# A bf16 matmul with scale and add on one core: a semaphore for each transfer, programs without loops, another order of transfers, and the weight cast on its way in

## The chip, the core and the metric

The kernel runs on one core of a Trainium2 chip. The metric is the time on the device in microseconds (us) of one execution. A core has a tensor engine (PE), a vector engine (DVE), a scalar engine (ACT), GpSimd (POOL) and SyncE (SP), each with its own program, which wait for one another by semaphores; 16 DMA engines carry data between HBM and the on-chip memory. A transfer adds 16 to its semaphore when it is complete. Matrix products go to an accumulator memory (`mm`).

## The reference

```python
batch, m, k, n = 16, 512, 1024, 768
x: (16, 512, 1024) float32, weight: (1024, 768) float32, scale = 0.1, add_value: (16, 512, 768) float32
return (scale * np.matmul(x, weight) + add_value).astype(np.float32)
```

With the batch flattened, x has 8192 rows: 33.55 MB of x, 3.15 MB of weight and 25.17 MB of add_value are read, and 25.17 MB are written.

## The kernel before, in words

The 8192 rows are cut into T = 64 tiles of 128 rows. With G = 8 (L9), a group is 1024 consecutive rows, partition p of the chip's memory holds 8 consecutive rows of it, and tile t of a group is row t of each partition (L53 to L55). So a transfer of n tiles is, for each of the 128 partitions, one contiguous run of n rows: 4 KB a tile for x, 3 KB a tile for add_value and out.

Buffers: `xs` holds 16 tiles of x in fp32; `ao` 32 tiles of add_value, in which the result is formed and from which it is stored; `w_bf` the weight in bf16; `va` two buffers of four tiles of x in bf16; `xt` four tiles after the transpose; `mm` four accumulators.

Each tile goes through five steps:

- **SP** issues all transfers on its one queue, in the order of the list `STREAM` (L19): ("x", 8, 4) loads tiles 8 to 11 of x, "w" half of the weight, "a" add_value, "o" stores out. `sync_engine` (L87) walks the list; where a buffer must first come free, SP waits ahead of the issue, and all that follows in the list waits with it. An x load waits until ACT and POOL have moved the tiles whose slots it takes (`by_act`, `by_pool`, L109). The loads of add_value share one semaphore `a_sem`, so each of them waits until the one before has landed (L117); four tiles at 52 have `a_late`. A load into a slot from which an earlier result is stored waits for that store (L122), a store for DVE's results (`made`, L133). The entry "m" (L97) makes four transfers of under 2 KB into a tile that nothing reads. The last store, tiles 56 to 63, is issued after all engines are through (L225).
- **ACT and POOL** (`mover`, L139) cast x from fp32 to bf16 into `va`, a move of four tiles at a time, each engine half of the partitions' data in 8 instructions (L152). A move waits for its load and until the turns of the move two before are done (`turned`). The 16 moves are a hardware loop of four rounds of four.
- **DVE** (`vector_engine`, L155) first casts the two halves of the weight, which were loaded as fp32 into `ao`, into `w_bf` (`cast_w`, L158). Then for each pair of tiles it transposes (`turn`, L162) from `va` into `xt`, and later does `finish` (L172): ao = mm * scale + ao, both tiles of the pair in one instruction. The order is turn 0, turn 1, then finish p, turn p + 2, and so on, in a hardware loop over groups. `turn` waits for both movers, `finish` for the products (`done`) and, at the start of a group, for add_value.
- **PE** (`tensor_engine`, L198) waits for the whole weight (`casts`, L202) before anything else, then multiplies: for each tile 16 matmuls, 8 blocks of k by two pieces of n (512 and 256 columns), in a hardware loop over four tiles. A pair waits for its turn and for an accumulator that has been read. 32 pairs are 1024 matmuls.

The weight stands second and third in `STREAM`, right behind the first four tiles of x.

Of the kernel before, what the change touches and what calls it, by code (L numbers as in the profile page):

```python
# [6 lines left out]

P = 128
G = 8  # L9
X_SLOTS = 16  # L10
A_SLOTS = 32
CUT = 512
MM_BUFS = 4
XT_TILES = 4
VA_BUFS = 2
MOVE = 4
AHEAD = 4

STREAM = [  # L19
# [5 lines left out]
]  # L25
LAST = (56, 8)
MARKS = [15, 8, 7, 1]


@with_exitstack  # L30
def kernel(
# [8 lines left out]
    nc = tc.nc  # L40
# [6 lines left out]
    M, K = x_f.shape  # L47
    _, N = weight.shape
    T = M // P
    KC = K // (2 * P)  # L50
    KJ = 2 * KC

# [5 lines left out]
    def rows(view, s, n):  # L58
# [10 lines left out]
    xt = const.tile([P, XT_TILES, KC, P], fp32, name="xt")  # L69
    mm = psum.tile([P, MM_BUFS, 1024], fp32, name="mm")  # L70

    marks = const.tile([P, len(MARKS), 16 * len(MARKS)], fp32, name="marks")
    mark = tc.alloc_semaphore("mark")
    w_sem = [tc.alloc_semaphore(f"w{i}") for i in range(2)]
    x_sem = [tc.alloc_semaphore(f"x{i}") for i in range(X_SLOTS // MOVE)]
    a_sem, a_late = (tc.alloc_semaphore(n) for n in ("a", "a_late"))
    o_sem = [tc.alloc_semaphore(f"o{i}") for i in range(2)]
    by_act, by_pool, pool_go, turned, casts, done, made = (
        tc.alloc_semaphore(name)
        for name in ("by_act", "by_pool", "pool_go", "turned", "casts", "done", "made"))  # L80
    TURNED = MOVE * VA_BUFS
    MADE = TURNED + 2 + MM_BUFS - 2

    def slot(t):
        return (t + G) % A_SLOTS

    def sync_engine(eng):  # L87
        loads, stores, known = [], [], {}

        def need(sem, value):  # L90
            if known.get(sem, 0) < value:
                eng.wait_ge(sem, value)  # L92
                known[sem] = value

        for op, s, n in STREAM:
            last = s + n - 1
            if op == "m":  # L97
                for i, k in enumerate(MARKS):
                    eng.dma_start(marks[0:k, i, 0:16 * (i + 1)],  # L99
                                  w_v[0:k, 0, 0:16 * (i + 1)]).then_inc(mark, 16)  # L100
                continue
            if op == "w":
                dst = ao[:, s:s + n, :].rearrange("p (c r) n -> p c (r n)", r=2)
                move, sem = eng.dma_start(dst, w_v[:, s // 2:(s + n) // 2, :]), w_sem[s // 4]  # L104
            elif op == "x":
                k = s % X_SLOTS
                if last >= X_SLOTS:
                    moved = 8 * (last + 1 - X_SLOTS) // MOVE
                    need(by_act, moved)  # L109
                    need(by_pool, moved)  # L110
                    if n == 2 * MOVE:
                        eng.sem_inc(x_sem[k // MOVE + 1], 16)  # L112
                move = eng.dma_start(xs[:, k:k + n, :], rows(x_v, s, n))  # L113
                sem = x_sem[k // MOVE]
            elif op == "a":
                if loads:
                    need(a_sem, 16 * len(loads))  # L117
                if slot(s) == 0:
                    need(casts, KJ)
                if s >= A_SLOTS:  # L120
                    i = next(j for j, (a, b) in enumerate(stores) if a <= s - A_SLOTS < a + b)
                    need(o_sem[i % 2], 16 * (i // 2 + 1))  # L122
                move = eng.dma_start(ao[:, slot(s):slot(s) + n, :], rows(add_v, s, n))  # L123
                if s % G:
                    sem = a_late
                else:
                    sem = a_sem
                    loads.append((s, n))
            else:
                i = len(stores)  # L130
                if i > 1:
                    need(o_sem[i % 2], 16 * (i // 2))
                need(made, MADE + last + 1)  # L133
                move = eng.dma_start(rows(out_v, s, n), ao[:, slot(s):slot(s) + n, :])
                sem = o_sem[i % 2]
                stores.append((s, n))
            move.then_inc(sem, 16)

    def mover(eng, copy, parity, count, go=None):  # L139
        if go is None:  # L140
            eng.preload_act_table(mybir.ActivationFunctionType.Copy)  # L141
        with eng.Fori(16, 16 * (T // X_SLOTS) + 1, 16) as i:
            for q in range(X_SLOTS // MOVE):
                eng.wait_ge(x_sem[q], i)
                eng.wait_ge(turned, i + (4 * q - 12) if q < 3 else i)  # L145
                if go is not None:
                    eng.sem_inc(go, 1)  # L147
                k = MOVE * q
                src = xs[:, k:k + MOVE, :].rearrange("p i (c b k) -> p (i c) b k", b=4, k=64)
                for a in (parity, parity + 2):  # L150
                    for b in range(4):
                        copy(va[q % VA_BUFS][32 * b:32 * b + 32, :, a, :],  # L152
                             src[32 * a:32 * a + 32, :, b, :]).then_inc(count, 1)

    def vector_engine(eng):  # L155
        ao_g = ao.rearrange("p (g t) n -> p g t n", t=G)

        def cast_w(s, n):  # L158
            eng.wait_ge(w_sem[s // 4], 16)
            eng.tensor_copy(w_bf[:, s:s + n, :], ao[:, s:s + n, :]).then_inc(casts, n)  # L160

        def turn(move, half, moves=None):  # L162
            if half == 0:
                eng.wait_ge(by_act, moves)
                eng.wait_ge(by_pool, moves)
            q = 2 * half * KC
            eng.transpose(  # L167
                xt[:, 2 * half:2 * half + 2, :, :].rearrange("p i c m -> p (i c m)"),
                va[move % VA_BUFS][:, q:q + 2 * KC, :, :].bitcast(fp32).rearrange("p c a k -> p (c a k)"),
            ).then_inc(turned, 2)  # L170

        def finish(pair, at, products):  # L172
            eng.wait_ge(done, products)
            a = ao_g[:, at, 2 * pair:2 * pair + 2, :]
            q = 2 * (pair % 2)
            eng.scalar_tensor_tensor(  # L176
                a, mm[:, q:q + 2, 0:N], float(scale), a,
                op0=mybir.AluOpType.mult, op1=mybir.AluOpType.add).then_inc(made, 2)

        def group(i, at, last):  # L180
            eng.wait_ge(a_sem, i)
            for p in range(4):
                if p == 2 and not last:
                    eng.wait_ge(a_late, i)
                finish(p, at, i + (4 * p - 12) if p < 3 else i)
                if p < 2 or not last:
                    turn(1 if p < 2 else 0, p % 2, i + 8 if p == 2 else i)

        cast_w(0, 4)
        cast_w(4, 4)  # L190
        turn(0, 0, 8)
        turn(0, 1)
        with eng.Fori(16, 2 * T, 16) as i:
            group(i, bass.ds((i // 16) % (A_SLOTS // G), 1), False)
        s = slot(T - G) // G
        group(2 * T, slice(s, s + 1), True)

    def tensor_engine(eng):  # L198
        eng.sem_inc(turned, TURNED)
        eng.sem_inc(made, MADE)  # L200
        eng.sem_inc(a_late, 16 * (T // G - 2))
        eng.wait_ge(casts, KJ)  # L202
        with eng.Fori(TURNED + 2, TURNED + 2 + T, XT_TILES) as i:
            for q in range(XT_TILES):
                if q % 2 == 0:
                    eng.wait_ge(turned, i + q if q else i)
                    eng.wait_ge(made, i + q if q else i)
                for j in range(KJ):
                    x2 = xt[:, q, j // 2, :].bitcast(bf16).rearrange("p (m r) -> p r m", r=2)
                    for n0, n1 in ((0, CUT), (CUT, N)):  # L210
                        m = eng.matmul(  # L211
                            mm[:, q, n0:n1], x2[:, j % 2, :], w_bf[:, j, n0:n1],
                            start=(j == 0), stop=(j == KJ - 1))
                if q % 2:
                    m.then_inc(done, 4)
        eng.wait_ge(mark, 16 * len(MARKS))

    with tc.tile_critical(no_gpsimd_drain=True):  # L218
        sync_engine(nc.sync)
# [1 line left out]
        mover(nc.gpsimd, nc.gpsimd.tensor_copy, 1, by_pool, pool_go)  # L221
        vector_engine(nc.vector)
        tensor_engine(nc.tensor)
    s, n = LAST
    nc.sync.dma_start(rows(out_v, s, n), ao[:, slot(s):slot(s) + n, :])  # L225


# [33 lines left out]
```

## Time and profile before

| what | us |
|---|---|
| median of 3 runs (lowest, highest) | 215.4 (215.06, 215.68) |
| profiled execution, first to last instruction (its span) | 213.8 |
| PE busy with matmuls | 172.2 |
| ACT, POOL busy | 134.7, 135.4 |
| DVE busy | 97.9 |

The profiled execution's own time is known as its span; what lies around the span is the rest to the run's time.

How to read the rows: a row of the timeline or of the chain begins with the start from the span's beginning and a length, both in us; then come the engine (SPq is SP's queue of instructions), the line of the kernel and the operation, written as output<-input, with the number of instructions xN; in square brackets stands how long the engine had been idle before, and what released it. A row of a group of instructions has, after the bars, the busy time and the mean of one in nanoseconds, then the idle time before them. A row by stretch gives the busy time of each engine with the number of instructions in brackets. The granted clock is a share of TensorE's full clock.

### The profile page before, as it was taken

The numbers are of one execution on the slowest core, as the hardware profiler recorded it, in microseconds if no ns is written. First come the engines' busy times: TensorE is split into PE (matmuls) and PEld (weight loads), VectorE is DVE, ScalarE is ACT, GpSimd is POOL, SyncE is SP. The second block draws the span as 40 slices with busy tenths as digits, with TensorE's granted clock in tenths as the row PEclk, the third lists the DMA queues.
The fourth block names the chain that finished last, engine by engine and source line by source line (L and its number), as shares of the span: only waits on it lengthen the run. The fifth ranks groups of instructions, "written<-read, shape, count | busy, mean of one in ns | idle before, by whom it ended". The sixth has DMA issues, their size and how long they took to land.

```text
span 213.8 us, 2747 instructions
## 1 busy us (share of the span) xinstructions
PE 172.2 (81%) x1024; PEld 101.7 (48%) x1024; DVE 97.9 (46%) x66; ACT 134.7 (63%) x129; POOL 135.4 (63%) x132
## 2 busy tenths in 40 slices
PE   0000999999999999999999999999989906999800
PEld 0000455656566665656566665656546503556400
DVE  0046245565537555555555555555454307055310
ACT  2492947993799999896932999199900599600000
POOL 0398957994699999996932999199910499700000
PEclk9999999999999999999999999999999975799965
DMA  6999999999999999999999999999849999999766
GB/s 233 409 437 441 441 395 463 432 451 417 428 455 392 447 435 392 463 395 441 437 418 438 443 458 423 418 437 432 382 149 434 435 432 368 441 437 432 308 294 294
DMA packets 4782, 87.04 MB, mean 407 GB/s; under 512 B 558, under 2 KB 558, under 8 KB 1070
## 3 DMA queue, kind: packets, MB, share of 16 engines
q1 hardware_dynamic: 4782, 87.04, 96.1%
HBM read 61.87 MB, written 25.17 MB: 407 GB/s over the span
## 4 chain that ended last, share of the span: by engine, by line
DMA 63%; POOL 15%; PE 11%; issue 2%; SPq 2%; DVE 1%; POOLq 0%; DVEq 0%
DMA out_dram<-ao 26%; DMA xs<-in_x_dram 25%; POOL va L152 15%; DMA ao<-in_add_value_dram 12%; PE mm L211 11%; DVE ao L176 1%; SPq L99 1%; DVE xt L167 1%; SPq L113 0%; SPq L104 0%; SPq L123 0%; POOLq L145 0%; SPq L112 0%; POOLq L147 0%; SPq L92 0%
## 5 line engine op out<-in xcount | busy, mean ns | idle before, releaser
L211 PE MATMUL mm<-w_bf,xt 128*128 128x512 bf16 (+1 forms) x1024 | 172.2, 332 | 29.9 <-DVE xt L167 29.9
L152 POOL CAST va<-xs 32x1024 bf16<-32x1024 f32 x128 | 135.2, 1056 | 50.1 <-DMA xs<-in_x_dram 41.4
L152 ACT CAST va<-xs 32x1024 bf16<-32x1024 f32 x128 | 133.5, 1043 | 49.6 <-DMA xs<-in_x_dram 44.0
L211 PEld LDWEIGHTS mm<-w_bf,xt 128*128 128x128 bf16 x1024 | 101.7, 100 | 100.0 <-DVE xt L167 30.6
L176 DVE SCALAR_TENSOR_TENSOR ao<-mm,ao 128x1536 f32 (+1 forms) x32 | 56.2, 1756 | 77.7 <-PE mm L211 72.7
L167 DVE STREAM_TRANSPOSE xt<-va 128x1024 f32<-128x1024 f32 x32 | 39.5, 1235 | 14.7 <-POOL va L152 14.7
L160 DVE CAST w_bf<-ao 128x3072 bf16<-128x3072 f32 x2 | 4.5, 2228 | 13.7 <-DMA ao<-in_weight_dram 13.7
L141 ACT ACT_TABLE_LOAD x1 | 1.3, 1283 | 0.9 <-SPq L218 0.9
L242 POOL MEMSET const-float32-0.0<- 128x1 f32 x1 | 0.1, 98 | 0.2 <-issue 0.2
L242 POOL MEMSET const-bfloat16-1.0<- 128x1 bf16 x1 | 0.1, 100 | 0.0
L242 POOL MEMSET const-float32-1.0<- 128x1 f32 x1 | 0.1, 98 | 0.0
L242 POOL MEMSET const-uint8-127<- 128x1 uint8 x1 | 0.1, 98 | 0.0
## 6 DMA issues: line engine op xcount, KB each, us to landing
out_dram<-ao SPq DMA_DIRECT2D x8, 3072.0 KB, 29.3
ao<-in_add_value_dram SPq DMA_DIRECT2D x7, 3072.0 KB, 17.1
xs<-in_x_dram SPq DMA_DIRECT2D x8, 2048.0 KB, 18.8
xs<-in_x_dram SPq DMA_DIRECT2D x4, 4096.0 KB, 23.1
ao<-in_weight_dram SPq DMA_DIRECT2D x2, 1536.0 KB, 12.4
ao<-in_add_value_dram SPq DMA_DIRECT2D x2, 1536.0 KB, 8.7
marks<-in_weight_dram SPq DMA_DIRECT2D x1, 0.9 KB
marks<-in_weight_dram SPq DMA_DIRECT2D x1, 1.0 KB
```

What stands on the lines that cost most here:

```text
L99: eng.dma_start(marks[0:k, i, 0:16 * (i + 1)], w_v[0:k, 0, 0:16 * (i + 1)]).then_inc(mark, 16)
L141: eng.preload_act_table(mybir.ActivationFunctionType.Copy)
L152: copy(va[q % VA_BUFS][32 * b:32 * b + 32, :, a, :], src[32 * a:32 * a + 32, :, b, :]).then_inc(count, 1)
L160: eng.tensor_copy(w_bf[:, s:s + n, :], ao[:, s:s + n, :]).then_inc(casts, n)
L167: eng.transpose(xt[:, 2 * half:2 * half + 2, :, :].rearrange("p i c m -> p (i c m)"), va[move % VA_BUFS][:, q:q + 2 * KC, :, :].bitcast(fp ...
L176: eng.scalar_tensor_tensor(a, mm[:, q:q + 2, 0:N], float(scale), a, op0=mybir.AluOpType.mult, op1=mybir.AluOpType.add).then_inc(made, 2)
L211: m = eng.matmul(mm[:, q, n0:n1], x2[:, j % 2, :], w_bf[:, j, n0:n1], start=(j == 0), stop=(j == KJ - 1))
L242: nc = _bacc.Bacc("TRN2", target_bir_lowering=False, num_devices=1)
```

## The change

- The list becomes a string: "x4+8" loads tiles 4 to 11 of x. Each transfer but the last has its own semaphore (`landed`), and whoever needs the data waits for the transfers that carry it (`carriers`). SP waits for moves, for stores out of slots that a load takes, and for results; it no longer waits for a load.
- G is 16: partitions hold 16 consecutive rows of a group of 2048, and a transfer of 16 tiles is possible. The new order has x in transfers of eight tiles but for two, one load of add_value and one store with 16 tiles, and a last store of four tiles (60 to 63).
- The weight leaves `STREAM`. GpSimd issues two transfers, ahead of all its casts, that read fp32 and write bf16 into `w_bf`. DVE's casts go; PE waits for the two transfers. `ao` no longer holds the weight, so slots are counted from 0.
- The four small transfers "m" go.
- ACT, POOL and DVE have their programs written out in place of the loops; a wait that an earlier wait of the same engine covers is left out. PE keeps its loop.

```diff
@@ -6,7 +6,7 @@
 from concourse._compat import with_exitstack
 
 P = 128
-G = 8
+G = 16
 X_SLOTS = 16
 A_SLOTS = 32
 CUT = 512
@@ -14,17 +14,17 @@
 XT_TILES = 4
 VA_BUFS = 2
 MOVE = 4
-AHEAD = 4
-
-STREAM = [
-    ("x", 0, 4), ("w", 0, 4), ("w", 4, 4), ("x", 4, 4), ("a", 0, 8),
-    ("x", 8, 4), ("x", 12, 4), ("a", 8, 8), ("x", 16, 8), ("a", 16, 8), ("x", 24, 8),
-    ("a", 24, 8), ("x", 32, 8), ("m", 0, 4), ("o", 0, 8), ("o", 8, 8), ("a", 32, 8), ("x", 40, 4),
-    ("x", 44, 4), ("a", 40, 8), ("x", 48, 8), ("o", 16, 8), ("o", 24, 8), ("a", 48, 4), ("a", 52, 4),
-    ("x", 56, 4), ("x", 60, 4), ("a", 56, 8), ("o", 32, 8), ("o", 40, 8), ("o", 48, 8),
-]
-LAST = (56, 8)
-MARKS = [15, 8, 7, 1]
+
+STREAM = """
+    x0+4 x4+8 a0+8 a8+8 x12+4 x16+8 a16+16 x24+8 o0+8 x32+8 o8+8 a32+8 x40+8 a40+8 x48+8
+    o16+8 o24+8 a48+4 x56+8 a52+4 a56+8 o32+16 o48+4 o52+8 o60+4
+"""
+
+
+def transfers():
+    for word in STREAM.split():
+        s, n = word[1:].split("+")
+        yield word[0], int(s), int(n)
 
 
 @with_exitstack
@@ -47,6 +47,7 @@
     M, K = x_f.shape
     _, N = weight.shape
     T = M // P
+    MOVES = T // MOVE
     KC = K // (2 * P)
     KJ = 2 * KC
 
@@ -69,137 +70,119 @@
     xt = const.tile([P, XT_TILES, KC, P], fp32, name="xt")
     mm = psum.tile([P, MM_BUFS, 1024], fp32, name="mm")
 
-    marks = const.tile([P, len(MARKS), 16 * len(MARKS)], fp32, name="marks")
-    mark = tc.alloc_semaphore("mark")
+    stream = list(transfers())
+    landed = [tc.alloc_semaphore(f"{op}{s}") for op, s, n in stream[:-1]]
     w_sem = [tc.alloc_semaphore(f"w{i}") for i in range(2)]
-    x_sem = [tc.alloc_semaphore(f"x{i}") for i in range(X_SLOTS // MOVE)]
-    a_sem, a_late = (tc.alloc_semaphore(n) for n in ("a", "a_late"))
-    o_sem = [tc.alloc_semaphore(f"o{i}") for i in range(2)]
-    by_act, by_pool, pool_go, turned, casts, done, made = (
+    by_act, by_pool, pool_go, turned, done, made = (
         tc.alloc_semaphore(name)
-        for name in ("by_act", "by_pool", "pool_go", "turned", "casts", "done", "made"))
+        for name in ("by_act", "by_pool", "pool_go", "turned", "done", "made"))
     TURNED = MOVE * VA_BUFS
-    MADE = TURNED + 2 + MM_BUFS - 2
-
-    def slot(t):
-        return (t + G) % A_SLOTS
+    MADE = TURNED + MM_BUFS
+
+    def carriers(op, s, n):
+        return [sem for (o, a, k), sem in zip(stream, landed)
+                if o == op and a < s + n and s < a + k]
+
+    def slots(op, s, n):
+        ring = X_SLOTS if op == "x" else A_SLOTS
+        k = s % ring
+        assert k + n <= ring
+        return slice(k, k + n)
+
+    def engine(eng):
+        known = {}
+
+        def need(sem, value):
+            if known.get(sem.num if hasattr(sem, "num") else id(sem), 0) < value:
+                eng.wait_ge(sem, value)
+                known[sem.num if hasattr(sem, "num") else id(sem)] = value
+
+        return need
+
+    def transfer(eng, op, s, n):
+        if op == "x":
+            return eng.dma_start(xs[:, slots(op, s, n), :], rows(x_v, s, n))
+        if op == "a":
+            return eng.dma_start(ao[:, slots(op, s, n), :], rows(add_v, s, n))
+        return eng.dma_start(rows(out_v, s, n), ao[:, slots(op, s, n), :])
 
     def sync_engine(eng):
-        loads, stores, known = [], [], {}
-
-        def need(sem, value):
-            if known.get(sem, 0) < value:
-                eng.wait_ge(sem, value)
-                known[sem] = value
-
-        for op, s, n in STREAM:
-            last = s + n - 1
-            if op == "m":
-                for i, k in enumerate(MARKS):
-                    eng.dma_start(marks[0:k, i, 0:16 * (i + 1)],
-                                  w_v[0:k, 0, 0:16 * (i + 1)]).then_inc(mark, 16)
-                continue
-            if op == "w":
-                dst = ao[:, s:s + n, :].rearrange("p (c r) n -> p c (r n)", r=2)
-                move, sem = eng.dma_start(dst, w_v[:, s // 2:(s + n) // 2, :]), w_sem[s // 4]
-            elif op == "x":
-                k = s % X_SLOTS
-                if last >= X_SLOTS:
-                    moved = 8 * (last + 1 - X_SLOTS) // MOVE
-                    need(by_act, moved)
-                    need(by_pool, moved)
-                    if n == 2 * MOVE:
-                        eng.sem_inc(x_sem[k // MOVE + 1], 16)
-                move = eng.dma_start(xs[:, k:k + n, :], rows(x_v, s, n))
-                sem = x_sem[k // MOVE]
-            elif op == "a":
-                if loads:
-                    need(a_sem, 16 * len(loads))
-                if slot(s) == 0:
-                    need(casts, KJ)
+        need = engine(eng)
+        for (op, s, n), sem in zip(stream, landed):
+            last = s + n
+            if op == "x" and last > X_SLOTS:
+                moved = 8 * -(-(last - X_SLOTS) // MOVE)
+                need(by_act, moved)
+                need(by_pool, moved)
+            if op == "a":
                 if s >= A_SLOTS:
-                    i = next(j for j, (a, b) in enumerate(stores) if a <= s - A_SLOTS < a + b)
-                    need(o_sem[i % 2], 16 * (i // 2 + 1))
-                move = eng.dma_start(ao[:, slot(s):slot(s) + n, :], rows(add_v, s, n))
-                if s % G:
-                    sem = a_late
-                else:
-                    sem = a_sem
-                    loads.append((s, n))
-            else:
-                i = len(stores)
-                if i > 1:
-                    need(o_sem[i % 2], 16 * (i // 2))
-                need(made, MADE + last + 1)
-                move = eng.dma_start(rows(out_v, s, n), ao[:, slot(s):slot(s) + n, :])
-                sem = o_sem[i % 2]
-                stores.append((s, n))
-            move.then_inc(sem, 16)
+                    for old in carriers("o", s - A_SLOTS, n):
+                        need(old, 16)
+            if op == "o":
+                need(made, MADE + last)
+            transfer(eng, op, s, n).then_inc(sem, 16)
 
     def mover(eng, copy, parity, count, go=None):
+        need = engine(eng)
         if go is None:
             eng.preload_act_table(mybir.ActivationFunctionType.Copy)
-        with eng.Fori(16, 16 * (T // X_SLOTS) + 1, 16) as i:
-            for q in range(X_SLOTS // MOVE):
-                eng.wait_ge(x_sem[q], i)
-                eng.wait_ge(turned, i + (4 * q - 12) if q < 3 else i)
-                if go is not None:
-                    eng.sem_inc(go, 1)
-                k = MOVE * q
-                src = xs[:, k:k + MOVE, :].rearrange("p i (c b k) -> p (i c) b k", b=4, k=64)
-                for a in (parity, parity + 2):
-                    for b in range(4):
-                        copy(va[q % VA_BUFS][32 * b:32 * b + 32, :, a, :],
-                             src[32 * a:32 * a + 32, :, b, :]).then_inc(count, 1)
+        else:
+            half = KC // len(w_sem)
+            for i, sem in enumerate(w_sem):
+                eng.dma_start(
+                    w_bf[:, 2 * half * i:2 * half * (i + 1), :].rearrange("p (c r) n -> p c (r n)", r=2),
+                    w_v[:, half * i:half * (i + 1), :]).then_inc(sem, 16)
+        for q in range(MOVES):
+            for sem in carriers("x", MOVE * q, MOVE):
+                need(sem, 16)
+            if q >= VA_BUFS:
+                need(turned, TURNED + MOVE * (q - VA_BUFS + 1))
+            if go is not None:
+                eng.sem_inc(go, 1)
+            k = MOVE * q % X_SLOTS
+            src = xs[:, k:k + MOVE, :].rearrange("p i (c b k) -> p (i c) b k", b=4, k=64)
+            for a in (parity, parity + 2):
+                for b in range(4):
+                    copy(va[q % VA_BUFS][32 * b:32 * b + 32, :, a, :],
+                         src[32 * a:32 * a + 32, :, b, :]).then_inc(count, 1)
 
     def vector_engine(eng):
-        ao_g = ao.rearrange("p (g t) n -> p g t n", t=G)
-
-        def cast_w(s, n):
-            eng.wait_ge(w_sem[s // 4], 16)
-            eng.tensor_copy(w_bf[:, s:s + n, :], ao[:, s:s + n, :]).then_inc(casts, n)
-
-        def turn(move, half, moves=None):
-            if half == 0:
-                eng.wait_ge(by_act, moves)
-                eng.wait_ge(by_pool, moves)
+        need = engine(eng)
+
+        def turn(pair):
+            move, half = divmod(pair, 2)
+            need(by_act, 8 * (move + 1))
+            need(by_pool, 8 * (move + 1))
+            if pair > 1:
+                need(done, 4 * (pair - 1))
             q = 2 * half * KC
             eng.transpose(
                 xt[:, 2 * half:2 * half + 2, :, :].rearrange("p i c m -> p (i c m)"),
                 va[move % VA_BUFS][:, q:q + 2 * KC, :, :].bitcast(fp32).rearrange("p c a k -> p (c a k)"),
             ).then_inc(turned, 2)
 
-        def finish(pair, at, products):
-            eng.wait_ge(done, products)
-            a = ao_g[:, at, 2 * pair:2 * pair + 2, :]
+        def finish(pair):
+            for sem in carriers("a", 2 * pair, 2):
+                need(sem, 16)
+            need(done, 4 * (pair + 1))
+            a = ao[:, slots("a", 2 * pair, 2), :]
             q = 2 * (pair % 2)
             eng.scalar_tensor_tensor(
                 a, mm[:, q:q + 2, 0:N], float(scale), a,
                 op0=mybir.AluOpType.mult, op1=mybir.AluOpType.add).then_inc(made, 2)
 
-        def group(i, at, last):
-            eng.wait_ge(a_sem, i)
-            for p in range(4):
-                if p == 2 and not last:
-                    eng.wait_ge(a_late, i)
-                finish(p, at, i + (4 * p - 12) if p < 3 else i)
-                if p < 2 or not last:
-                    turn(1 if p < 2 else 0, p % 2, i + 8 if p == 2 else i)
-
-        cast_w(0, 4)
-        cast_w(4, 4)
-        turn(0, 0, 8)
-        turn(0, 1)
-        with eng.Fori(16, 2 * T, 16) as i:
-            group(i, bass.ds((i // 16) % (A_SLOTS // G), 1), False)
-        s = slot(T - G) // G
-        group(2 * T, slice(s, s + 1), True)
+        turn(0)
+        turn(1)
+        for pair in range(T // 2):
+            finish(pair)
+            if pair + 2 < T // 2:
+                turn(pair + 2)
 
     def tensor_engine(eng):
         eng.sem_inc(turned, TURNED)
         eng.sem_inc(made, MADE)
-        eng.sem_inc(a_late, 16 * (T // G - 2))
-        eng.wait_ge(casts, KJ)
+        for sem in w_sem:
+            eng.wait_ge(sem, 16)
         with eng.Fori(TURNED + 2, TURNED + 2 + T, XT_TILES) as i:
             for q in range(XT_TILES):
                 if q % 2 == 0:
@@ -213,7 +196,6 @@
                             start=(j == 0), stop=(j == KJ - 1))
                 if q % 2:
                     m.then_inc(done, 4)
-        eng.wait_ge(mark, 16 * len(MARKS))
 
     with tc.tile_critical(no_gpsimd_drain=True):
         sync_engine(nc.sync)
@@ -221,8 +203,7 @@
         mover(nc.gpsimd, nc.gpsimd.tensor_copy, 1, by_pool, pool_go)
         vector_engine(nc.vector)
         tensor_engine(nc.tensor)
-    s, n = LAST
-    nc.sync.dma_start(rows(out_v, s, n), ao[:, slot(s):slot(s) + n, :])
+    transfer(nc.sync, *stream[-1])
 
 
 # ---- launch: one core; inputs and outputs as the reference has them ----
```

## The prediction

> **What bounds the kernel now.** I read the page first (span, busy time, DMA queue, chain), then the busy time by stretch, then the chain and the timeline at the start and at the end.
>
> ```profile
> span 213.8 us, 2747 instructions
> PE 172.2 (81%) x1024; PEld 101.7 (48%) x1024; DVE 97.9 (46%) x66; ACT 134.7 (63%) x129; POOL 135.4 (63%) x132
> DMA packets 4782, 87.04 MB, mean 407 GB/s; under 512 B 558, under 2 KB 558, under 8 KB 1070
> q1 hardware_dynamic: 4782, 87.04, 96.1%
> DMA 63%; POOL 15%; PE 11%; issue 2%; SPq 2%; DVE 1%; POOLq 0%; DVEq 0%
> ```
>
> One queue moves 87.04 MB at 96% of the 16 DMA engines' time, and the chain is 63% DMA: the stream of transfers bounds the kernel, with TensorE (81%) second. The packet counts tell what a packet is. Between 2 and 8 KB there are 1070 - 558 = 512 packets, and the weight has 2 transfers x 128 partitions x 2 rows = 512 runs of 6 KB; above 8 KB there are 4782 - 1070 = 3712, and the 29 transfers of x, add_value and out have 29 x 128 = 3712 runs. So a packet is one contiguous run of one partition: 16 KB for four tiles of x, 32 KB for eight, 24 KB for eight of add_value or out. Each engine gets 128 / 16 = 8 of them for a transfer.
>
> By stretch (columns: engines' busy time and instructions, granted clock, DMA share, GB/s):
>
> ```profile
> 0.00:2.50 2.50, 0.00 (x0) 0.00 (x0) 0.00 (x0) 1.28 (x1) 0.20 (x4) 1.00 0.44 92
> 2.50:9.00 6.50, 0.00 (x0) 0.00 (x0) 0.00 (x0) 0.56 (x1) 0.42 (x1) 1.00 0.90 378
> 9.00:28.00 19.00, 6.46 (x24) 3.17 (x25) 6.83 (x4) 14.78 (x15) 17.34 (x15) 1.00 1.02 435
> 28.00:73.00 45.00, 45.00 (x279) 27.14 (x278) 25.07 (x17) 35.67 (x35) 35.11 (x35) 1.00 1.01 433
> ...
> 145.00:155.00 10.00, 10.00 (x63) 6.02 (x62) 4.99 (x4) 9.78 (x10) 9.46 (x10) 1.00 0.94 404
> 155.00:161.00 6.00, 5.35 (x33) 3.05 (x32) 3.79 (x3) 0.20 (x1) 0.73 (x1) 1.00 0.54 176
> 161.00:200.00 39.00, 31.32 (x178) 17.94 (x176) 15.28 (x11) 16.68 (x16) 16.55 (x16) 0.87 1.01 424
> 200.00:205.00 5.00, 2.09 (x14) 1.05 (x11) 1.76 (x1) 0.00 (x0) 0.00 (x0) 0.94 0.37 157
> 205.00:213.80 8.80, 0.00 (x0) 0.00 (x0) 0.00 (x0) 0.00 (x0) 0.00 (x0) 0.50 0.84 357
> ```
>
> Full rate is 433 GB/s; 87.04 MB / 433 = 201.0 us. The other 12.8 us are time lost at less than that rate, (1 - rate/433) x length: head 2.0 + 0.8, 145 to 155 0.7, **155 to 161 3.6**, 161 to 200 0.8, **200 to 205 3.2**, end 1.5, together 12.6. The two holes in bold have these causes:
>
> ```profile
> SPq L123 <- DMA ao<-in_add_value_dram: 67.7, 5, 23.6
> ```
>
> ```profile
> 145.70 11.17 DMA ao<-in_add_value_dram
> ...
> 157.33 10.75 DMA xs<-in_x_dram
> ```
>
> SP is held at L123 until the add_value load before has landed (L117, the shared semaphore). At 145.70 it issues tiles 48 to 51 and then stands until they land at 156.87; the queue runs dry, and the x tiles 56 to 59, issued at 157.33, land at 168.08. TensorE starves on them:
>
> ```profile
> 160.18 10.58 PE L211 MATMUL mm<-w_bf,xt 128*128 128x512 bf16 x64 [0.65 <-DVE xt L167]
> 178.44 23.65 PE L211 MATMUL mm<-w_bf,xt 128*128 128x512 bf16 x128 [7.68 <-DVE xt L167]
> 197.00 1.76 DVE L176 SCALAR_TENSOR_TENSOR ao<-mm,ao 128x1536 f32<-128x1536 f32 x1 [2.29 <-PE mm L211]
> 202.20 1.76 DVE L176 SCALAR_TENSOR_TENSOR ao<-mm,ao 128x1536 f32<-128x1536 f32 x1 [3.44 <-PE mm L211]
> 204.24 0.33 SPq L225 DMA_DIRECT2D out_dram<-ao  x1
> ```
>
> ```profile
> 175.00:180.00 5.00, 1.56 (x5) 0.74 (x6) 2.87 (x3) 4.88 (x6) 4.76 (x5) 0.50 0.96 339
> 180.00:185.00 5.00, 5.00 (x20) 2.50 (x19) 1.17 (x2) 4.90 (x5) 4.70 (x6) 0.61 1.05 452
> ```
>
> It idles 0.65 and 7.68 us, then runs slowly after the pause (20 matmuls in 5 us where 33 are usual, clock 0.50 and 0.61). The last store waits for it: that is the hole at 200. And the start:
>
> ```profile
> 8.44 8.51 ACT L152 CAST va<-xs 32x1024 bf16<-32x1024 f32 x8 [6.25 <-DMA xs<-in_x_dram]
> 8.58 11.52 POOL L152 CAST va<-xs 32x1024 bf16<-32x1024 f32 x8 [8.14 <-DMA xs<-in_x_dram]
> 12.20 2.31 DVE L160 CAST w_bf<-ao 128x3072 bf16<-128x3072 f32 x1 [12.20 <-DMA ao<-in_weight_dram]
> 15.96 2.15 DVE L160 CAST w_bf<-ao 128x3072 bf16<-128x3072 f32 x1 [1.45 <-DMA ao<-in_weight_dram]
> 20.99 8.69 POOL L152 CAST va<-xs 32x1024 bf16<-32x1024 f32 x8 [0.88 <-DMA xs<-in_x_dram]
> 21.54 23.81 PE L211 MATMUL mm<-w_bf,xt 128*128 128x512 bf16 x129 [21.54 <-DVE xt L167]
> 29.79 1.76 DVE L176 SCALAR_TENSOR_TENSOR ao<-mm,ao 128x1536 f32 x1 [7.18 <-PE mm L211]
> ```
>
> **Two lengths decide the new kernel.** TensorE's: let S be its first matmul. The first finish (L176) comes 29.79 - 21.54 = 8.25 later, the other 31 at 5.20 apart (202.20 - 197.00) if nothing is late: S + 169.45; finish 1.76; to the last store's issue 0.28 (204.24 - 203.96); from there to the end 9.59 for eight tiles (213.83 - 204.24). The new last store has four tiles, 1.57 MB / 433 = 3.63 less: 5.96. So **span = S + 177.4**. For before, S = 21.54 with eight tiles gives 202.6; the missing 11.2 are the two idle times and the slow stretch.
> The stream's: 201.0 + head 2.8 + end 1.5 = **205.3** if the queue never runs dry. The larger wins; they cross at S = 27.9.
>
> **The change part by part.**
> *Own semaphores and order* remove the wait at L117. I went through SP's new list with the durations above: each wait is met while earlier transfers still have work queued. The tightest: tiles 48 to 51 of add_value wait for out 16 to 23, with out 24 to 31 (3.15 MB, 7.3 us) still queued. The holes at 155 and 200 go, 6.8 us of stream. Late next is x 56 to 63: 69.7 MB into the stream, it lands at 3.5 + 161 = 164.5 (3.5 because the first 2.10 MB, 4.84 us, were there at 8.4). Move 8.7, turn 1.25 (below), four pairs 20.8, finish, store 8.0: 203.3, or 206 if the clock falls again. So the stream's end is 205.3 to 206; I take 206.
>
> ```profile
> L167 DVE STREAM_TRANSPOSE xt<-va 128x1024 f32<-128x1024 f32 x32 | 39.5, 1235 | 14.7 <-POOL va L152 14.7
> ```
>
> *Written-out programs, no marks*: the loops' register work lies in the chain's issue share, 2% or 4.3 us at the very most. Fetching longer programs shows in no row; the nearest is what POOL loses between the casts of a move, 8.69 - 8 x 1.056 (L152, below) = 0.24, and doubled in 16 moves that is 3.9. I take 0, between -4.3 and +3.9, since ACT and POOL are off the path in the forecast. Four marks transfers go: SP's time beside a full queue, 0. *G = 16* doubles the pitch of the partitions' rows. Transfers of half a pitch (9 to 28 us, 435 GB/s) ran like whole ones (433): 0.
> *DVE's two casts* (2.31 + 2.15) go, and with them POOL's slow first move: 11.52 against 8.69, 2.8 us. Both lie ahead of TensorE's start and are worth something only if the weight is there.
> *The weight* leaves SP's queue for GpSimd's. Issuing costs POOL something that no row shows, but POOL idles 8.14 us ahead of its first cast, so 0 up to there. Moving it: the engines read the same 3.15 MB, 7.3 us at 433. By its written bytes it is 3.6, and if they converted at POOL's pace (L152, 32x1024 in 1.056 us by its group, so 786,432 elements in 25.3) it is 25. I take 7.3, the same bytes read by the same engines.
>
> ```profile
> L152 POOL CAST va<-xs 32x1024 bf16<-32x1024 f32 x128 | 135.2, 1056 | 50.1 <-DMA xs<-in_x_dram 41.4
> ```
>
> *When it lands* decides. Before, it stood second and third in SP's list and was there at 12.2 and 15.9. Now it has 32 runs of 6 KB per engine on a queue of its own, beside x 0+4, x 4+8, a 0+8, a 8+8 and x 12+4, which SP issues at once with no wait. If an engine takes one packet from each queue in turn, the 32 small runs go beside 32 large ones, four transfers of 8: 2.10 + 4.19 + 3.15 + 3.15 = 12.58 MB. The weight is complete after 15.73 MB, at 3.5 + 36.3 = 39.8, and a little later as GpSimd's queue will start later than SP's: 40.5. TensorE waits for both halves ahead of all its work (w_sem), and the whole engine is behind that wait: S = 40.5; the first tiles, landed at about 10, are turned long before. Span = 40.5 + 177.4 = 217.9. As a sum from before: +19.0 start, -11.2 end waits, -3.6 last store: +4.1. The stream then has 12 us of room. SP's loads of x wait for moves, these for turns (va has two buffers), these for TensorE; but x 24 to 31, let go by the fourth move at about S + 25 = 65.5, land at some 79 and are wanted by TensorE at S + 3 + 12 x 5.2 = 106, so the late start doesn't starve it afterwards.
>
> No row here has two queues at work; the sharing is the unknown of this forecast. The Trainium skill, DMA: Bandwidth & Descriptors, under SWDGE vs HWDGE vs iDMA, says that a packet is preferably at most 4096 B and is the boundary at which an engine changes queues; with runs of 6 KB and more that is one run for each turn, as forecast.
>
> **Rivals.**
> 1. *The weight comes early, and the kernel gets faster.* An engine takes from a queue all the packets that one transfer left it, or shares by bytes. In turns of whole transfers the order is x 0+4, first half, x 4+8, second half: 9.43 MB, S about 3.5 + 21.8 = 25.3 and then the first turn is not late: under 27.9, the stream decides, span 206. It decides from S = 27.9 down, and S below 36.4 is faster than before. For it: nothing in the trace says that runs are the unit of sharing. Against: the runs are what the engines' records count. The same page, under Queues, rings and completion order, says that an engine drains a whole packet, typically 9 to 17 descriptors, before it changes; 8 or 16 runs and one for the semaphore are 9 and 17, and by that reading this rival holds. No run shows it yet.
> 2. *The cast is slow.* At 25.3 us instead of 7.3 the stream grows by 18: span 224 with rival 1, 236 with the forecast's sharing. Shorter pieces than a run, one for each large one, would be worse. Against: the transfer reads no more than the plain one.
> 3. *The stream's holes stay*, or the longer programs start moves late, and the weight is early: about 213, no change.
>
> **How the numbers follow.** The median of the runs, 215.4, lies 1.6 above the profiled span; I add 1.6. Forecast 217.9 + 1.6 = 219.5, chance 0.52; its own range is 215.9 (weight at its written bytes) to 223.5 (GpSimd's queue starting some microseconds late). Rival 1: 207.6, 0.32. Rival 2: 225 and up, 0.10. Rival 3: 0.06. Range 205.5 to 223.5. About 0.3% (0.65 us) is what a measurement of this kernel can tell from no change. Slower: forecast, rival 2 less a little, 0.61; faster: rival 1 and part of rival 3, 0.35; same 0.04.
>
> **What would show it.** First matmul at 40 (right) or 25 (rival 1). A second queue of 512 packets in the DMA part, and its rows' time against the plain weight's. No idle time of TensorE longer than 1 us after the start, and finishes 5.20 apart to the end (right); PE waiting for x 56 to 63 near 170 (rival 1). No wait of SP at the add_value lines for a load. DMA share below 0.9 in most stretches (right) or 1.0 throughout (rival 1).

## The result, and the profile after

The changed kernel takes 221.94 us (median of 4 runs, 221.30 to 222.54), the kernel before in the same comparison 215.23: a ratio of 1.032, interval 1.028 to 1.035. It is slower by 3.2%. The forecast was 219.5.

The profiled execution took 222.54 us, with a span of 220.8. From its page, the span, the busy time, the transfers and the chain that ended last:

```profile
span 220.8 us, 2630 instructions
PE 169.5 (77%) x1024; PEld 101.1 (46%) x1024; DVE 93.2 (42%) x64; ACT 134.7 (61%) x129; POOL 134.5 (61%) x134
DMA packets 4147, 85.49 MB, mean 387 GB/s; under 512 B 432, under 2 KB 432, under 8 KB 944
q1 hardware_dynamic: 3600, 83.89, 90.7%
q0 software_dynamic: 544, 1.57, 3.6%
PE 77%; DMA 18%; DVE 1%; issue 1%; POOL 0%; POOLq 0%; DVEq 0%; SPq 0%
```

The bound has changed: the chain was 63% DMA and is 77% PE. The weight appears as a second queue, q0, with its 944 - 432 = 512 runs, counted by the 1.57 MB that it writes. Its 3.6% of 220.8 us are 7.9 us of the engines' time, near the 7.3 that its 3.15 MB read cost at 433 GB/s. So the cast itself is not dear.

The chain in order of time (start, length, what; all but some pieces under 0.7 us):

```profile
1.46 0.83 POOL w_bf L132
2.29 40.24 DMA w_bf<-in_weight_dram
42.53 0.48 issue
43.01 169.52 PE mm L194 x1024
...
212.62 1.76 DVE ao L170
```

The weight is issued at 1.46 us and is there at 42.53; from 43.01 TensorE multiplies without a pause for 169.52 us. The waits say the same, for TensorE and for SP's queue:

```profile
PE mm L194 <- DMA w_bf<-in_weight_dram: 43.0, 1, 43.0
```

```profile
SPq L97 <- POOL va L146: 123.1, 5, 37.7
SPq L107 <- DVE ao L170: 43.4, 3, 20.4
SPq L106 <- DMA out_dram<-ao: 25.4, 3, 20.1
```

SP no longer waits for a load of add_value (67.7 us before), but 123.1 us for moves, which wait for turns, which wait for TensorE. SP's queue runs dry in the middle (from 88 to 92 us the engines move 143 GB/s), and nobody misses the time, since TensorE is busy throughout. The finishes (L170) at the start and at the end:

```profile
18.18 2.37 DVE L159 STREAM_TRANSPOSE xt<-va 128x1024 f32<-128x1024 f32 x2 [18.18 <-POOL va L146]
...
43.01 37.23 PE L194 MATMUL mm<-w_bf,xt 128*128 128x512 bf16 x210 [43.01 <-DMA w_bf<-in_weight_dram]
51.45 1.76 DVE L170 SCALAR_TENSOR_TENSOR ao<-mm,ao 128x1536 f32<-128x1536 f32 x1 [30.91 <-PE mm L194]
...
212.62 1.76 DVE L170 SCALAR_TENSOR_TENSOR ao<-mm,ao 128x1536 f32<-128x1536 f32 x1 [3.44 <-PE mm L194]
```

The first tiles are turned at 20.6 and lie there for 22 us. The 31 finishes behind the first are (212.62 - 51.45) / 31 = 5.20 us apart. And by stretch, where the stream has room (371 and 241 GB/s, where 433 is its full rate) and, between them, where it has none:

```profile
73.00:112.00 39.00, 39.00 (x242) 23.48 (x241) 22.52 (x16) 30.82 (x31) 30.71 (x31) 1.00 0.95 371
112.00:145.00 33.00, 33.00 (x205) 19.81 (x204) 17.45 (x12) 26.83 (x27) 26.62 (x26) 1.00 1.00 428
...
200.00:214.00 14.00, 12.51 (x78) 7.34 (x75) 6.05 (x4) 0.00 (x0) 0.00 (x0) 1.00 0.56 241
```

### The profile page after: what moved, and what is told of

Read it like the earlier page. It is cut to its first block, busy times and chain, and to the rows that moved or that the text cites. A ratio compares the mean times of both kernels' runs of the same rounds, so it can differ in the third digit from the quotient of the medians.

```text
span 220.8 us, 2630 instructions
## 1 busy us (share of the span) xinstructions
PE 169.5 (77%) x1024; PEld 101.1 (46%) x1024; DVE 93.2 (42%) x64; ACT 134.7 (61%) x129; POOL 134.5 (61%) x134
## 3 DMA queue, kind: packets, MB, share of 16 engines
q0 software_dynamic: 544, 1.57, 3.6%
## 4 chain that ended last, share of the span: by engine, by line
PE 77%; DMA 18%; DVE 1%; issue 1%; POOL 0%; POOLq 0%; DVEq 0%; SPq 0%
PE mm L194 77%; DMA w_bf<-in_weight_dram 18%; DVE ao L170 1%; POOL w_bf L132 0%; POOLq L237 0%; DVEq L97 0%; SPq L200 0%
## 5 line engine op out<-in xcount | busy, mean ns | idle before, releaser
L194 PE MATMUL mm<-w_bf,xt 128*128 128x512 bf16 (+1 forms) x1024 | 169.5, 329 | 43.0 <-DMA w_bf<-in_weight_dram 43.0
L146 POOL CAST va<-xs 32x1024 bf16<-32x1024 f32 x128 | 132.8, 1037 | 57.5 <-DVE xt L159 32.9
L170 DVE SCALAR_TENSOR_TENSOR ao<-mm,ao 128x1536 f32<-128x1536 f32 x32 | 56.3, 1759 | 103.0 <-PE mm L194 103.0
L159 DVE STREAM_TRANSPOSE xt<-va 128x1024 f32<-128x1024 f32 x32 | 39.4, 1234 | 18.2 <-POOL va L146 18.2
L132 POOL DMA_DIRECT2D w_bf<-in_weight_dram x2 | 1.6, 777 | 1.0 <-SPq L200 1.0
```

Of the source, the lines that this page charges most:

```text
L132: eng.dma_start(w_bf[:, 2 * half * i:2 * half * (i + 1), :].rearrange("p (c r) n -> p c (r n)", r=2), w_v[:, half * i:half * (i + 1), :]). ...
L146: copy(va[q % VA_BUFS][32 * b:32 * b + 32, :, a, :], src[32 * a:32 * a + 32, :, b, :]).then_inc(count, 1)
L159: eng.transpose(xt[:, 2 * half:2 * half + 2, :, :].rearrange("p i c m -> p (i c m)"), va[move % VA_BUFS][:, q:q + 2 * KC, :, :].bitcast(fp ...
L170: eng.scalar_tensor_tensor(a, mm[:, q:q + 2, 0:N], float(scale), a, op0=mybir.AluOpType.mult, op1=mybir.AluOpType.add).then_inc(made, 2)
L194: m = eng.matmul(mm[:, q, n0:n1], x2[:, j % 2, :], w_bf[:, j, n0:n1], start=(j == 0), stop=(j == KJ - 1))
```

## The experiments

The theory (T): the DMA engines take one contiguous run from each of the two queues in turn, so the weight's 32 small runs per engine wait for 32 large ones. Rivals: the cast itself is slow (R1); GpSimd's queue gets a fixed small share beside SP's (R2); something else in the change costs. The trace has one record for each run, with its start, and these records test T directly: how many of SP's runs start between the first and the last of the weight's 512?

| kernel | weight's runs from, to (us) | SP's runs between | their MB |
|---|---|---|---|
| changed kernel | 6.0 to 41.4 | 472 | 11.9 |
| small runs beside the weight | 5.8 to 19.8 | 481 | 2.5 |
| large runs beside it | 5.8 to 49.7 | 477 | 15.7 |
| before, weight issued by GpSimd | 6.0 to 33.9 | 475 | 8.8 |

The bytes differ six times over; the runs are always a little under 512. With the 4-byte records that end a transfer counted on both sides, SP's queue has 536 to 545 against 533 to 537. Equal counts alone would also come from turns of eight runs each. The order of the records speaks against that: at no moment between the first and the last run is one queue more than 10 records ahead of the other, over all 16 engines together. If engines that start together took eight runs at a turn, one queue would be ahead by up to 128. The order also repeats itself after 32 records, two for each of the 16 engines: a record and the one 32 places behind it are of the same queue in 67 to 76% of the cases, against 30 to 54% at 8, 16 or 24 places. The records do not name their engine, so the turn of one run is inferred from this. The four kernels follow; those with large runs and with GpSimd issuing in the kernel before were run once.

**Small runs.** In the changed kernel's list:

```diff
-    x0+4 x4+8 a0+8 a8+8 x12+4 ...
+    x0+4 x4+1 x5+1 x6+1 x7+1 x8+4 a0+8 a8+8 x12+4 ...
```

> Theory T: an engine takes one run from each of the two queues in turn, so what stands beside the weight's 32 runs decides when it is there. Here the load of x tiles 4 to 11 is cut into four of one tile (runs of 4 KB) and one of four; the 32 runs beside the weight are then mostly small ones. By T the weight is complete after x 0+4, the four single tiles and a little of x 8+4: about 20 to 22 us instead of 42.5; first matmul near 21, span near 208 (the stream is then the bound), time near 209.7. Rival R1, the cast itself is slow (some 36 us of the engines' time whatever runs beside it): weight still at 42, span 220 or more. Rival R2, the queue of GpSimd gets a fixed small share (3.15 MB in 36 us, 87 GB/s) beside SP's: also still 42, span 220.

210.65 us; against before 0.978 (0.974 to 0.982). Span 209.1. The timeline at the start, and the last moves of x, of which more below:

```profile
18.20 2.37 DVE L159 STREAM_TRANSPOSE xt<-va 128x1024 f32<-128x1024 f32 x2 [18.20 <-POOL va L146]
21.05 11.86 PE L194 MATMUL mm<-w_bf,xt 128*128 128x512 bf16 x63 [21.05 <-DVE xt L159]
...
167.22 17.05 ACT L146 CAST va<-xs 32x1024 bf16<-32x1024 f32 x16 [11.23 <-DMA xs<-in_x_dram]
```

The first matmul starts at 21.05 us instead of 43.01, with the same two casting transfers on the same queue, and the kernel is faster than before. It waits for the turn (L159) now, no longer for the weight. R1 and R2, by which the weight would still come at 42, fall.

**Large runs.** The opposite:

```diff
-    x0+4 x4+8 a0+8 a8+8 x12+4 x16+8 a16+16 x24+8 ...
+    x0+4 x4+8 a0+16 x12+4 a16+16 x16+8 x24+8 ...
```

> The opposite of the small runs: the first loads of add_value have 16 tiles (runs of 48 KB) in place of eight (24 KB), with as many runs. T: beside the weight's 32 runs stand x 0+4, x 4+8, a 0+16, x 12+4 and most of a 16+16; the weight is complete after 22.4 MB more or less, at 54 to 56 us; first matmul near 56, span near 234, time near 236. R1 and R2: weight at 42 as in the changed kernel, span near 221 (the order of the loads behind the start hardly matters then).

231.5 us, span 229.7. Its chain:

```profile
2.29 49.83 DMA w_bf<-in_weight_dram
52.12 0.48 issue
```

The weight is there at 52.1, not 42.5, for nothing but longer runs beside it; 2 us earlier than the low end of what was expected. S + 177.4 with S = 52.6 is 230.0, against a span of 229.7.

**The kernel before, with the weight issued by GpSimd.** Plain fp32 transfers, DVE casts:

```diff
-    ("x", 0, 4), ("w", 0, 4), ("w", 4, 4), ("x", 4, 4), ("a", 0, 8),
+    ("x", 0, 4), ("x", 4, 4), ("a", 0, 8),
...
+        else:
+            for s, n in ((0, 4), (4, 4)):
+                dst = ao[:, s:s + n, :].rearrange("p (c r) n -> p c (r n)", r=2)
+                eng.dma_start(dst, w_v[:, s // 2:(s + n) // 2, :]).then_inc(w_sem[s // 4], 16)
```

> The kernel before with one edit: the weight's two transfers, plain fp32 into the same place, are issued by GpSimd ahead of its casts instead of by SP; DVE casts as before. No cast in a transfer. T: the 32 runs go beside the last of x 0+4, x 4+4, a 0+8, x 8+4 and most of x 12+4 (14.2 MB with the weight), so the second half lands at about 36 to 38 us, DVE's cast adds 2.2, first matmul near 39 to 40, span near 221, time near 222.5. R1 (the cast is what is slow): the weight shares the queue and is there by about 20 us, span as before, 214. R2 (fixed small share): weight at 42, first matmul 45, span 226.

221.0 us, against before 215.31; span 219.0. The start:

```profile
35.32 1.76 DVE L161 CAST w_bf<-ao 128x3072 bf16<-128x3072 f32 x1 [12.07 <-DMA ao<-in_weight_dram]
37.00 2.37 DVE L168 STREAM_TRANSPOSE xt<-va 128x1024 f32<-128x1024 f32 x2
38.29 21.90 PE L212 MATMUL mm<-w_bf,xt 128*128 128x512 bf16 x121 [38.29 <-DVE xt L168]
```

There is no cast in a transfer here, and the loops and shared semaphores are those of the kernel before; yet 5.7 us of the changed kernel's loss of 6.7 are there. So the queue is the cause. The first matmul comes at 38.3, a little ahead of T's 39 to 40, and the time is 1.5 us less than expected. The start is 16.8 us later than before and costs only 5.7, since little is left of the 11.2 us that TensorE lost later in the kernel before, in two pauses and a slow stretch: it idles 0.4 us after its start.

**The weight alone on the engines.** SP is held after its first transfer:

```diff
+            if (op, s) == ("x", 4):
+                for w in w_sem:
+                    need(w, 16)
```

> The changed kernel with one edit: SP waits for both halves of the weight after it has issued x 0+4, so that GpSimd's queue has the engines to itself. This measures the casting transfers alone. T, with the cast at the price of the bytes it reads: 3.15 MB in 7.3 us, so complete at about 15 to 16 us; first matmul near 19.5 (the first move and turn are then the bound), the queue loses 2 to 3 us until x 4+8 starts, TensorE waits some 5 us for it; span near 208, time near 209.7. R1: the weight lands at 40 or later and the stream behind it starts then, span 235 or more. R2: like T.

212.8 us; against before 0.989 (0.986 to 0.992). Span 211.0, some 3 us more than expected. Its chain begins

```profile
2.29 13.24 DMA w_bf<-in_weight_dram
16.94 30.32 DMA xs<-in_x_dram
```

so the casting transfers, with little beside them, are complete at 15.5, as expected: the cast runs at the price of its reads. It also shows the price of holding: the next rows of x start after 16.9, and the moves of x 56 to 63 at 169.3, some 2 us later than with small runs (167.2). The span is longer by as much; the other 1.1 us also delay the kernel with small runs, which was expected at 208 and ends at 209.1.

**The weight's part alone undone.** SP loads the weight as fp32 into slots of add_value, DVE casts it, and the load of 16 tiles is split in two, so that the slots are free in time. Core of the edit:

```diff
-    x0+4 x4+8 a0+8 a8+8 x12+4 x16+8 a16+16 x24+8 ...
+    x0+4 w0+4 w4+4 x4+8 a0+8 a8+8 x12+4 x16+8 a16+8 a24+8 x24+8 ...
...
+        for s in (0, 4):
+            need(*carriers("w", s, 4), 16)
+            eng.tensor_copy(w_bf[:, s:s + 4, :], ao[:, 24 + s:28 + s, :]).then_inc(casts, 4)
...
-        for sem in w_sem:
-            eng.wait_ge(sem, 16)
+        eng.wait_ge(casts, KJ)
```

> The changed kernel with the weight's part alone undone: two plain transfers on SP's queue behind x 0+4, into slots 24 to 31 of ao, cast by DVE; add_value 16+16 becomes 16+8 and 24+8, the second behind the casts. Semaphores, written-out programs and order stay. Theory T (all of the loss is the weight's lateness): weight landed at 12 and 16 as before, first matmul near 21.5, then bound by the stream, span 207.5 to 209.5, time 209 to 211, so the rest of the change is worth some 5 us. Rival (the rest of the change costs too, longer programs or the doubled pitch): first matmul at 21.5 as well, but span 214 or more.

210.19 us; against before (215.37) 0.977 (0.973 to 0.982). Span 208.7:

```profile
21.52 12.31 PE L194 MATMUL mm<-w_bf,xt 128*128 128x512 bf16 x63 [21.52 <-DVE xt L157]
...
177.78 22.65 PE L194 MATMUL mm<-w_bf,xt 128*128 128x512 bf16 x126 [3.72 <-DVE xt L157]
```

Everything else in the change together is worth 5.2 us (215.37 - 210.19); the weight's part costs 11.8 (221.94 - 210.19) on top of it.

**The pitch.** The kernel with small runs, with

```diff
-G = 16
+G = 8
...
-    x0+4 x4+1 x5+1 x6+1 x7+1 x8+4 a0+8 a8+8 x12+4 x16+8 a16+16 x24+8 ...
+    x0+4 x4+1 x5+1 x6+1 x7+1 x8+4 a0+8 a8+8 x12+4 x16+8 a16+8 a24+8 x24+8 ...
...
-    ... o32+16 o48+4 o52+8 o60+4
+    ... o32+8 o40+8 o48+8 o56+4 o60+4
```

> The kernel with small runs beside the weight, and G = 8 instead of 16; the two transfers of 16 tiles become pairs of eight and the last stores 48+8, 56+4, 60+4. It tries the doubled pitch of the partitions' rows alone. If the pitch costs nothing, as the prediction has it: within 1 us of the small runs with G = 16 (210.65). If the pitch is why that kernel's stream moves 425 to 435 GB/s: 2 to 4 us faster, and its rates between 45 and 180 us 1 to 2% higher.

210.37 us; against before 0.978 (0.974 to 0.982). Span 208.5. With G = 16, then with G = 8, by stretch:

```profile
45.00:73.00 28.00, 27.84 (x172) 16.88 (x173) 16.09 (x12) 25.03 (x24) 24.88 (x24) 1.00 1.01 435
73.00:112.00 39.00, 38.79 (x237) 23.26 (x240) 21.16 (x15) 31.29 (x30) 30.10 (x30) 1.00 1.00 428
```

```profile
45.00:73.00 28.00, 27.84 (x171) 16.88 (x173) 15.89 (x12) 25.03 (x24) 24.82 (x24) 1.00 1.00 431
73.00:112.00 39.00, 38.79 (x237) 23.36 (x240) 21.37 (x15) 31.46 (x31) 30.29 (x30) 1.00 1.00 429
```

The time lies 0.3 us from that with small runs and G = 16 (210.65), and the rates differ by 1% at most. The pitch costs nothing here.

**The price of the wait for a load.** The kernel before, with

```diff
-    ... ("a", 48, 4), ("a", 52, 4),
+    ... ("a", 48, 8),
...
-        eng.sem_inc(a_late, 16 * (T // G - 2))
+        eng.sem_inc(a_late, 16 * (T // G - 1))
```

> The kernel before with one edit: the add_value loads 48+4 and 52+4, of which the second waits for the first to land, are one load of eight. It tries the price of that wait alone. By the prediction's ledger the hole at 155 to 161 (3.6 us) goes, x 56 to 63 land 2.5 to 3.5 us earlier, and TensorE's idle time of 7.7 us shrinks by as much; the end is late by the same chain, so span 210 to 211.5, time 212 to 213. If the wait was hidden: 215.

210.75 us; against before 0.979 (0.975 to 0.982). Span 209.3, over 1 us better than expected. The stretch of the hole, and TensorE's pause:

```profile
155.00:161.00 6.00, 3.88 (x24) 2.16 (x22) 0.27 (x1) 0.05 (x1) 0.63 (x1) 1.00 0.97 418
```

```profile
163.70 33.85 PE L211 MATMUL mm<-w_bf,xt 128*128 128x512 bf16 x189 [4.76 <-DVE xt L167]
```

418 GB/s where there were 176. The long pause of 7.68 us before the last four pairs is gone; one of 4.76 remains, earlier, up to 163.70, where DVE waits 9.1 us for the merged load. One merged load (and the count that goes with it) gives what all of the change but the weight gives. Whether the semaphores by themselves would, with the loads left as they were, was not tried apart.

## Why the prediction was right, point by point

- **The weight's lateness** was the deciding step, and the runs bear it out: one run from each queue in turn. No row of before had two queues at work, so this choice was the prediction's open bet (0.52); it came out by the mechanism that was named, not by errors that cancelled. Predicted: complete at 40.5 after 15.73 MB; measured 42.53 after 16.61.
- **The size was 2.5 us too small**, all in S. The prediction let GpSimd's queue start "a little later" than SP's and took 0.7 us for it. The weight's first run starts at 6.0, SP's at 2.0. By then SP has started 94 of the 128 runs of x 0+4, so 54 runs of x 12+4 stand beside the weight instead. The sum with 16.61 MB gives 41.9, 1.4 us more than 40.5; the release of TensorE at 42.53 is 0.6 behind that, and the first matmul another 0.5 (the chain's issue), for which the sum had no term.
- **Span = S + 177.4** held: 43.01 + 177.4 = 220.4 against 220.8. The first finish came after 8.44 us (8.25), the others at 5.20, as said; from the end of the last finish to the end of the span 6.4 (6.24).
- **Nothing starves TensorE afterwards**: 1024 matmuls in one piece of 169.52 us. The clock did not fall again.
- **One sign did not show**: a DMA share below 0.9 in most stretches. It is 0.95 to 1.04 in the eight stretches from 2.5 to 200 us, below 0.9 only at the two ends. The prediction's own sum spoke against this sign: 201.0 us of transfers in a span of 217.9 are 0.92 on average. The share counts the time that records take, and the 32 KB runs took 1291 ns on average, where they took 1217 before; the room shows in the GB/s.
- **The cast's price**, 7.3 taken between 3.6 and 25: 7.9 in the records. Rival 2 was wrong. POOL's slow first move went with DVE's casts, as forecast: 8.71 us without them, 11.52 again where DVE casts (weight's part undone).
- **Rival 1** fell as a forecast, but is what the same program does once short runs stand beside the weight: 210.65 against its 207.6. The stream's floor of 205.3 to 206 was too low by some 3 us: four kernels of different build end at 208.5 to 209.3. In the stretches between 73 and 145 they move 425 to 431 GB/s, not 433 throughout, and each still has a pause of TensorE of 3.4 to 4.8 us in its second half. In the three with the new order the pause is the wait for x 56 to 63, which the prediction named as the next late ones. The sum had them there at 164.5; ACT's moves of them start at 166.6 to 167.5 (167.22 with small runs), which is 69.7 MB at 425 to 427 GB/s. From there to the end these kernels take 41.2 to 41.9 us, where the sum with the fallen clock had 41.5 (206 - 164.5). So in these three the 2 to 3 us lie in the stream ahead of x 56 to 63. Why it runs at some 426 and not 433 is open.
- **The rule of the Trainium skill** behind rival 1 (DMA: Bandwidth & Descriptors, Queues, rings and completion order: a whole packet of typically 9 to 17 descriptors before the engine changes queues) did not show here: with turns of whole transfers the weight would have come at about 25, and a lead of at most 10 records over 16 engines, in an order that repeats after 32, does not fit turns of 9 and more. The other sentence of the Trainium skill on that page, a packet of preferably at most 4096 B (SWDGE vs HWDGE vs iDMA), fits what the runs of 6 KB and more show, and those of 4 KB too.
- **The holes**: 6.8 us of stream were put down to 155 to 161 and 200 to 205; removing the first wait alone gave 4.6 us (215.37 - 210.75).
- **Nothing for pitch, loops and marks**: for the pitch shown. Kernels with loops (210.75) and written out (210.19) lie within 0.3% of each other, which leaves little for the programs; the two were not swapped alone.

## What to carry to other kernels

In these kernels GpSimd's queue did not get half of the engines' bytes beside SP's: it got one contiguous run for each run of SP's, so its small runs beside large ones crawled. What everything waits for belongs early in the same queue, or beside short runs. To estimate when it lands, count its runs per engine and add up the bytes of as many runs beside it. And when a stream is the bound, look for the one wait that lets its queue run dry before rebuilding the rest.

## What the runs showed of the hardware that was not expected

- GpSimd's queue began to move 4.5 us after its first issue (1.46 to 6.0 us, the same within 0.4 us in six kernels). The Trainium skill, DMA: Bandwidth & Descriptors, Latency and other measured facts, gives a first byte after some 1 us on this path; here it was later, with the two issues themselves taking 1.55 and SP's first load already running. What of the 4.5 us is due to that load was not tried.
- A transfer of GpSimd's that casts fp32 to bf16 and one that doesn't took the engines about the same time for a run: 247 and 235 ns for the same 6 KB read.
